# One pool for weights, sums and residual in a hybrid decoder layer, and five steps put elsewhere in the order

## The chip, the cores and the metric

The kernel runs on one core of a Trainium2 chip. The metric is the time of one execution on the device in microseconds; three executions of the kernel before gave a median of 2860.52 us (2858.32 to 2864.68).

## The reference

One decoder layer over 256 tokens of width 2048, all in float32. Shortened:

```
h = x + 1/2 * postN(SwiGLU_1(preN(x)))                  # D_FF = 5632
proj = preN(h) @ w_in  -> q | k | v | z | xBC | dt | gates
A = diff_attention(q, k, v)                             # 8 heads, causal, two softmax maps
S = mamba2(z, conv(xBC), softplus(dt + bias))           # 64 heads in 8 groups, chunks of 128
m = sigmoid(g_A) * (A @ w_branch_att) + sigmoid(g_S) * (S @ w_branch_ssm)
h = h + postN(m @ w_out)
h = h + 1/2 * postN(SwiGLU_2(preN(h)))
```

Every norm is an RMSNorm with a gain. Nearly all the work is products of 256 tokens with weights that are read once.

## The kernel before, in words

Tokens lie as two tiles of 128 (`NT = 2`). A float32 product is made of three matmuls on numbers that are split into a high and a low part: `split` (L109) takes a block of weights `raw`, ScalarE writes the high part `w_hi` (L122), VectorE subtracts it and writes the low part `w_lo` (L123). Activations are split in the same way into a "slot". `matmul3` and `prod` issue x_hi*w_hi, x_hi*w_lo, x_lo*w_hi.

Weights come in slabs of 1 MB, which are 8 KB on each of 128 partitions, on the queue of SyncE. The pool `raws` holds three of them, and `hpool` two further buffers of 8 KB: for the sums `wsum` in the two SwiGLUs, for `xv` and `dec` in the SSD groups, and for the residual `h` at the borders between the sub-layers. `wsplit` holds four high and four low parts of half a slab (and two of a quarter). A tile waits until its buffer's last readers are done.

**gate_up** (L338) makes one 512-wide slab of gate and up for one of the 11 values of `j`, out of eight slabs of weights, in the order `ORDER` or `ORDER_D`. Five of the eight are ordinary: two splits, 24 matmuls. The slabs 2, 4 and 6 (`SP`, from `j = 1` on) go a cheaper way, with 7 products (21 matmuls) in place of 8. That way needs four sums of quarters of the slab, which GpSimd makes (L366 to L369): s0 = r0+r3, s1 = r1+r3, s2 = s0+r1, s3 = s2+r2. They go into a tile `wsum` of their own, so they need no more than the landed slab. Four splits follow: a (quarters 0 and 1), d (quarter 2), b (s0, s1), c (s2, s3), and the products in the order p1 and u0 (from a), g0 (d), p5 and p7 (b), p6 and g1 (c); in the first such slab of a `gate_up`, u0 and g0 come later. After three values of `j` (the last time two), `project` multiplies with `w_down`.

The order on each engine is set when the program is built: a list scheduler simulates the engines and takes, of the ready instructions of an engine, the one of highest priority, which is the place in the program; `tc.high_priority(offset=AHEAD)` moves what it covers 300 places forward. All splits and sums stand under it. So an instruction whose input is late in that simulation lets later ones pass, TensorE's too; on the chip each engine keeps the order that was fixed.

**Borders.** After `w_down` and after `w_out`, `PostNorm.finish` (L271) updates `h` by quarters: token tile 0 at once, tile 1 through the returned `update(c)`. Then `h` is transposed into slots for the next projection. `queue` (filled in `pre_slots` and in the loop around L877) makes the third and fourth split behind a border issue after the first step of `update`.

**dt.** `decays` (L558) is a generator for dt and the decays of the SSM; `tick` runs it one step at a time after each projection. Its first step calls `rb()`, which spreads the row scale over the partitions with a matmul (L244, L245). **Merge.** For each n of `w_att`, the gated sum is transposed into a slot right behind the projection (`merged.append(to_slot(...))`).

Of the kernel before, what the change touches and what calls it, by code (L numbers as in the profile page):

```python
# [39 lines left out]
AHEAD = 300  # L40
# [12 lines left out]
def decoder_layer(ctx: ExitStack, tc: tile.TileContext, x, x_t, cols, rows, post_g, wgu1, wd1, w_in,  # L53
                  w_in_t, w_dt, w_att, w_ssm, w_out, wgu2, wd2, out):
    nc = tc.nc
    E = lambda **k: ctx.enter_context(tc.tile_pool(**k))
    const = E(name="const", bufs=1)
    raws = E(name="raws", bufs=3)
    wsplit = E(name="wsplit", bufs=4)
    slots = E(name="slots", bufs=9)  # L60
    big = E(name="big", bufs=1)
    hpool = E(name="hpool", bufs=2)
    tmp = E(name="tmp", bufs=12)
    small = E(name="small", bufs=4)
    psm = E(name="psm", bufs=8, space=bass.MemoryType.PSUM)
# [18 lines left out]
    h = None  # L84
    col = const.tile([P, NCOL], F32, name="col")
    nc.scalar.dma_start(col, cols)
    raw0 = raws.tile([P, 4, S], F32, name="raw")
    xT = big.tile([P, NP, 2, TT], F32, name="xT", tag="big")
    for b in range(2):
        nc.sync.dma_start(xT[:, b], x_t[b])  # L90
# [13 lines left out]
        nc.gpsimd.tensor_tensor(out=dst, in0=v[:, :k], in1=mhalf[:, :k], op=ALU.pow)  # L104

    loaded = [None]
    queue = []

    def split(raw, shape, parts=1, before=None):  # L109
        one = shape[1:] == [S]  # L110
        hi, lo = (wsplit.tile(shape, F32R, name=f"w_{p}", tag=f"w{p}{'1' if one else ''}", bufs=2 if one else None)
                  for p in ("hi", "lo"))
        k = shape[1] // parts
        with ExitStack() as st:
            st.enter_context(tc.high_priority(offset=AHEAD))
            for i in queue.pop(0) if queue else ():
                st.enter_context(tc.issue_after(i.ins))
            for a in range(0, shape[1], k):
                js = slice(a, a + k)
                if before:  # L120
                    before(js)
                nc.scalar.activation(hi[:, js], raw[:, js], AF.Copy)  # L122
                nc.vector.tensor_tensor(out=lo[:, js], in0=raw[:, js], in1=hi[:, js].bitcast(F32), op=ALU.subtract)  # L123
        return hi, lo
# [7 lines left out]
    def project(xs, w, n, by_token=0):  # L132

        ps = [psm.tile([P, S], F32, name="acc", tag="m") for _ in range(NT)]
        tail = []
        for c in range(len(xs)):
            raw = raws.tile([P, 4, S], F32, name="raw")
            loaded[0] = nc.sync.dma_start(raw, w(n, c))  # L140
            sl = xs[c] = xs[c]() if callable(xs[c]) else xs[c]
            for b in range(2):
                hi, lo = split(raw[:, 2 * b:2 * b + 2], [P, 2, S])
                for jj in range(2):
                    j = 2 * b + jj
                    tail.append((sl, j, hi[:, jj], lo[:, jj], c + j == 0, c == len(xs) - 1 and j == 3))
            if c < len(xs) - by_token:
                for sl_, j, wh, wl, first, last in tail:
                    for t in range(NT):
                        matmul3(ps[t], sl_, j, t, wh, wl, first, last)  # L150
                tail = []
        for t in range(NT):
            for sl_, j, wh, wl, first, last in tail:
                matmul3(ps[t], sl_, j, t, wh, wl, first, last)
        return ps

    def project_t(xs, w, n):

        ps = [psm.tile([P, 2 * TT], F32, name="acc", tag="m") for _ in range(2)]
        for b in range(len(xs)):  # L160
            if b % 2 == 0:
                raw = raws.tile([P, 8, 256], F32, name="raw")
                nc.sync.dma_start(raw, w(n, b // 2))
            hi, lo = split(raw[:, 4 * (b % 2):4 * (b % 2) + 4], [P, 4, 256])
            sl = xs[b].rearrange("p j i t -> p j (i t)")
# [172 lines left out]
    def gate_up(at, w, j, order, sp, rstd, fetch=None, after={}):  # L338
# [17 lines left out]
        for i, p in enumerate(order):  # L356
            raw = fetch(p) if fetch else None
            if raw is None:
                raw = raws.tile([P, 4, S], F32, name="raw")
                nc.sync.dma_start(raw, w[j, p])  # L360
            sl, k0 = at[p]
            if p in sp:

                e = hpool.tile([P, 4, S], F32, name="wsum", tag="h")
                with tc.high_priority(offset=AHEAD):
                    nc.gpsimd.tensor_tensor(out=e[:, 0], in0=raw[:, 0], in1=raw[:, 3], op=ALU.add)  # L366
                    nc.gpsimd.tensor_tensor(out=e[:, 1], in0=raw[:, 1], in1=raw[:, 3], op=ALU.add)
                    nc.gpsimd.tensor_tensor(out=e[:, 2], in0=e[:, 0], in1=raw[:, 1], op=ALU.add)
                    nc.gpsimd.tensor_tensor(out=e[:, 3], in0=e[:, 2], in1=raw[:, 2], op=ALU.add)  # L369
                ah, al = split(raw[:, 0:2], [P, 2, S])  # L370
                dh, dl = split(raw[:, 2], [P, S])
                bh, bl = split(e[:, 0:2], [P, 2, S])
                ch, cl = split(e[:, 2:4], [P, 2, S])
                seq = {"p1": (0, ah[:, 0], al[:, 0]), "u0": (6, ah[:, 1], al[:, 1]), "g0": (1, dh, dl),
                       "p5": (3, bh[:, 0], bl[:, 0]), "p7": (5, bh[:, 1], bl[:, 1]),
                       "p6": (4, ch[:, 0], cl[:, 0]), "g1": (2, ch[:, 1], cl[:, 1])}
                for k in (("p1", "p5", "p7", "p6", "u0", "g0", "g1") if i == units[0] else
                          ("p1", "u0", "g0", "p5", "p7", "p6", "g1")):
                    f, wh, wl = seq[k]
                    prod(k, sl[:, f, 0], sl[:, f, 1], wh, wl)  # L380
            else:
# [18 lines left out]
        out = []  # L400
# [110 lines left out]
    def rb():  # L511
        if not along:
            along.append(spread(rstd))
        return along[0]
# [7 lines left out]
    pending = []  # L522
# [17 lines left out]
        return v  # L540


    raw = raws.tile([P, 16, P], F32, name="raw")
    nc.sync.dma_start(raw, w_dt)
    pdt = psm.tile([P, 2 * TT], F32, name="pdt", tag="m")
    for c in range(2):
# [11 lines left out]
    def decays():  # L558
        dtT = tmp.tile([P, TT], F32, name="dtT", tag="t2")
        nc.scalar.activation(dtT, pdt[:, TT:], AF.Copy)  # L560
        nc.vector.tensor_tensor(out=dtT, in0=pdt[:, :TT], in1=dtT, op=ALU.add)
        nc.vector.tensor_tensor(out=dtT, in0=dtT, in1=rb()[:, 0], op=ALU.mult)
        pdv = psm.tile([P, NT, 64], F32, name="pdv", tag="m")
        for t in range(NT):
            nc.tensor.transpose(pdv[:, t], dtT[0:64, t * P:(t + 1) * P], ident[0:64, 0:64])
        yield
        nega = const.tile([P, 64], F32, name="nega")
        nc.scalar.activation(nega, row[:, 64:128], AF.Exp)
        nc.vector.tensor_scalar_mul(nega, nega, -1.0)
# [19 lines left out]
        nc.vector.scalar_tensor_tensor(out=dt, in0=dt, scalar=2.0, in1=v, op0=ALU.mult, op1=ALU.add)  # L589
        nc.vector.tensor_tensor(out=da, in0=dt, in1=nega.unsqueeze(1).broadcast_to([P, NT, 64]), op=ALU.mult)  # L590
        yield
        pcs = psm.tile([P, NT, 64], F32, name="pcs", tag="m")
        nc.tensor.matmul(pcs, tri, da, start=True, stop=True)
        nc.vector.tensor_copy(acs, pcs)
# [10 lines left out]
        for t in range(NT):  # L605
            nc.gpsimd.dma_start(acsD[t], acsT[:, t])

        yield
        lam = const.tile([P, 2], F32, name="lam")
        for i in range(2):  # L610
            c0 = C_LAM + 2 * i
# [5 lines left out]
        nc.vector.scalar_tensor_tensor(out=lamc, in0=elam[:, 0:1], scalar=LAMBDA_INIT, in1=elam[:, 1:2],  # L617
                                       op0=ALU.add, op1=ALU.subtract)

    pending.append(decays())  # L620
    subg = const.tile([P, 4], F32, name="subg")
    for i in range(2):
        nc.vector.tensor_scalar_mul(subg[:, 2 * i:2 * i + 2], col[:, C_SUB:C_SUB + 2], 1.0 - LAMBDA_INIT)
# [226 lines left out]

    merged, gates = [], {}
    gates[0], gates[1] = gate(W_GA), gate(W_GA + 1)
    for n in range(4):
        ps = project(att, lambda n, c: w_att[n, c], n)
        for t in range(NT):
            a = part[:, t, n * S:(n + 1) * S]
            nc.vector.tensor_tensor(out=gates[n][t], in0=ps[t], in1=gates[n][t], op=ALU.mult)
            nc.vector.tensor_tensor(out=a, in0=a, in1=gates[n][t], op=ALU.add)
        if n + 2 < 4:
            gates[n + 2] = gate(W_GA + n + 2)  # L860
        merged.append(to_slot([part[:, t, n * S:(n + 1) * S] for t in range(NT)]))

    h = [hpool.tile([P, D], F32, name=f"hb{t}", tag="h") for t in range(NT)]
    for t in range(NT):
# [81 lines left out]
```

## Time and profile before

| | before |
|---|---|
| median of three executions | 2860.52 us |
| the profiled execution, its own time | 2859.6 us |
| its span in the trace | 2857.9 us |
| TensorE busy | 2788.2 us, 98% |
| VectorE, ScalarE, GpSimd busy | 2035.1, 1442.8, 601.7 us |
| granted TensorE clock, mean | 0.992 |
| DMA, mean of 16 engines | 189 GB/s, 541.49 MB |

All times below are from this one execution, in microseconds from the start of the span. Matmuls are pipelined: a busy TensorE is not one at its peak, and a row of 512 columns is shown with 0.39 us though the next starts 0.227 us later. A wait for several semaphores is put down to the one that came last.

### The profile page before, as it was taken

The page shows a single profiled execution, that of the slowest core. Times are in us where ns is not written, and L with a number is a line of the kernel's source. Part 1 is how long each engine was busy: PE and PEld are TensorE (multiplying, and loading weights), DVE is VectorE, ACT ScalarE, POOL GpSimd, SP SyncE. Part 2 cuts the span into 40 slices and gives each one's busy share as a digit, 9 for nine tenths or more (in the row PEclk, how much of TensorE's full clock was granted, in tenths as well). Part 3 has the DMA queues.
Part 4 walks back from the last instruction along what each step waited for, and adds up shares of the span by engine and source line. Part 5 has one row for each costly group of instructions (what it writes and reads, how often), then busy time and mean ns, then how long its engine had stood idle before and what let it go on. Part 6 is the DMA issues. An engine that isn't in the chain of part 4 may idle for free. (4 is left out here: it accounts for less than half of the span.)

```text
span 2857.9 us, 33698 instructions
## 1 busy us (share of the span) xinstructions
PE 2788.2 (98%) x13120; PEld 2314.6 (81%) x13120; DVE 2035.1 (71%) x2311; ACT 1442.8 (50%) x1824; POOL 601.7 (21%) x377
## 2 busy tenths in 40 slices
PE   8999999999999999999999999999999999999998
PEld 6887887887778888888788888888878887887877
DVE  7858868778677886777665555545568679688686
ACT  6545545544555555545444444444455455455454
POOL 2415325233011120111100000000005145054150
PEclk9999999999999999999999999999999999999999
DMA  6555555556545554545545445555555554545555
GB/s 239 186 183 191 192 181 204 190 191 232 182 175 182 188 178 176 206 166 189 205 177 177 171 170 182 197 197 187 187 186 189 197 186 180 204 181 207 185 201 183
DMA packets 77984, 541.49 MB, mean 189 GB/s; under 512 B 8768, under 2 KB 8912, under 8 KB 14080
## 3 DMA queue, kind: packets, MB, share of 16 engines
q1 hardware_dynamic: 73152, 519.08, 50.3%
q0 software_dynamic: 4528, 20.09, 2.1%
q8 instruction: 103, 1.69, 0.2%
q14 instruction: 57, 0.47, 0.0%
q10 hardware_dynamic: 144, 0.17, 0.0%
HBM read 532.94 MB, written 6.36 MB: 189 GB/s over the span
## 5 line engine op out<-in xcount | busy, mean ns | idle before, releaser
L123 DVE TENSOR_TENSOR w_lo<-raw,w_hi 128x1024 fp32r<-128x1024 f32 (+1 forms) x978 | 1341.9, 1383 | 704.7 <-ACT w_hi L122 697.9
L122 ACT ACTIVATE w_hi<-raw 128x1024 fp32r<-128x1024 f32 (+1 forms) x978 | 1000.0, 1032 | 1073.6 <-PE acc L130 574.2
L128 PE MATMUL acc<-w_hi,slot 128*128 128x512 f32 x1856 | 731.0, 394 | 0.9 <-DVE y L685 0.3
L129 PE MATMUL acc<-w_lo,slot 128*128 128x512 f32 x1856 | 724.2, 390 | 0.0
L130 PE MATMUL acc<-w_hi,slot 128*128 128x512 f32 x1856 | 721.3, 390 | 0.0
L128 PEld LDWEIGHTS acc<-w_hi,slot 128*128 128x128 f32 x1856 | 349.5, 188 | 77.4 <-ACT slot L185 4.1
L169 PE MATMUL acc<-slot,w_hi 128*128 128x512 f32 x1280 | 408.7, 400 | 0.2 <-ACT zs L729 0.2
L129 PEld LDWEIGHTS acc<-w_lo,slot 128*128 128x128 f32 x1856 | 349.7, 188 | 73.1 <-issue 1.0
L130 PEld LDWEIGHTS acc<-w_hi,slot 128*128 128x128 f32 x1856 | 349.4, 188 | 73.0
L350 PE MATMUL gu<-w_lo,slot 128*128 128x512 f32 x928 | 366.0, 394 | 12.5 <-DVE w_lo L123 12.3
L349 PE MATMUL gu<-w_hi,slot 128*128 128x512 f32 x928 | 365.0, 394 | 7.1 <-ACT w_hi L122 7.1
L351 PE MATMUL gu<-w_hi,slot 128*128 128x512 f32 x928 | 363.0, 391 | 0.0
L171 PEld LDWEIGHTS acc<-slot,w_lo 128*128 128x128 f32 x1280 | 241.3, 189 | 56.4
L366 POOL TENSOR_TENSOR wsum<-raw 128x512 f32<-128x512 f32 x60 | 82.8, 1381 | 862.7 <-DMA raw<-in_wgu 836.3
L171 PE MATMUL acc<-slot,w_lo 128*128 128x256 f32 x1280 | 253.7, 279 | 0.0
L350 PEld LDWEIGHTS gu<-w_lo,slot 128*128 128x128 f32 x928 | 175.2, 189 | 57.6 <-DVE w_lo L123 22.7
L349 PEld LDWEIGHTS gu<-w_hi,slot 128*128 128x128 f32 x928 | 175.4, 189 | 45.8 <-ACT w_hi L122 7.5
L351 PEld LDWEIGHTS gu<-w_hi,slot 128*128 128x128 f32 x928 | 175.1, 189 | 35.9
L169 PEld LDWEIGHTS acc<-slot,w_hi 128*128 128x128 f32 x1280 | 197.5, 189 | 4.3 <-issue 2.4
L122 ACT ACTIVATE w_hi<-wsum 128x1024 fp32r<-128x1024 f32 x120 | 126.7, 1056 | 117.0 <-POOL wsum L369 50.5
L350 PE MATMUL gu<-w_lo,sums 128*128 128x512 f32 x420 | 165.4, 394 | 10.8 <-DVE w_lo L123 10.7
L123 DVE TENSOR_TENSOR w_lo<-wsum,w_hi 128x1024 fp32r<-128x1024 f32 x120 | 158.6, 1342 | 16.8 <-ACT w_hi L122 16.3
(229 smaller groups left out, 2354.5 us busy)
## 6 DMA issues: line engine op xcount, KB each, us to landing
raw<-in_wgu SPq DMA_DIRECT2D x175, 1024.0 KB, 4.8
raw<-in_wd SPq DMA_DIRECT2D x88, 1024.0 KB, 4.7
raw<-in_w_in SPq DMA_DIRECT2D x80, 1024.0 KB, 4.7
raw<-in_w_in_t SPq DMA_DIRECT2D x80, 1024.0 KB, 4.8
raw<-in_w_ssm SPq DMA_DIRECT2D x32, 1024.0 KB, 4.8
raw<-in_w_att SPq DMA_DIRECT2D x16, 1024.0 KB, 4.7
raw<-in_w_out SPq DMA_DIRECT2D x16, 1024.0 KB, 4.8
dec<-acsD POOLq DMA_DIRECT2D x16, 512.0 KB, 5.2
```

The lines of the kernel that those rows point to most:

```text
L122: nc.scalar.activation(hi[:, js], raw[:, js], AF.Copy)
L123: nc.vector.tensor_tensor(out=lo[:, js], in0=raw[:, js], in1=hi[:, js].bitcast(F32), op=ALU.subtract)
L128: nc.tensor.matmul(ps, xh, wh, start=first, stop=False)
L129: nc.tensor.matmul(ps, xh, wl, start=False, stop=False)
L130: nc.tensor.matmul(ps, xl, wh, start=False, stop=last)
L169: nc.tensor.matmul(ps[f], hi[:, j, wf[f]], sl[:, j], start=b + j == 0, stop=False)
L171: nc.tensor.matmul(ps[f][:, TT:], lo[:, j, wf[f]], sl[:, j, :TT], start=False, stop=b == len(xs) - 1 and j == 3)
L349: nc.tensor.matmul(bank[k], xh, wh, start=done[k] == 1, stop=False)
L350: nc.tensor.matmul(bank[k], xh, wl, start=False, stop=False)
L351: nc.tensor.matmul(bank[k], xl, wh, start=False, stop=done[k] == count[k])
L366: nc.gpsimd.tensor_tensor(out=e[:, 0], in0=raw[:, 0], in1=raw[:, 3], op=ALU.add)
```

## The change

`raws` is gone: its slabs come from `hpool`, which has five buffers for slabs, `xv`, `dec` and `h` together. In the slabs 2, 4 and 6 the sums are written over the slab itself, after its splits a and d, and in another order, so that split b reads quarters 0 and 1 again (p5, p6) and split c quarters 2 and 3 (g1, p7). `split` takes no high priority while `queue` holds something, that is for the first four splits behind each border. Of `decays`, the first step runs at once (`next(chain)`), the transposes of dtT come one step later, an empty step stands ahead of the cumulated sums, and the step ahead of lambda is gone. The transposes of the merged slab n come after the projection n+1, those of the last one inside the next projection.

```
-    raws = E(name="raws", bufs=3)
-    hpool = E(name="hpool", bufs=2)
+    hpool = E(name="hpool", bufs=5)
...
-    raw = raws.tile([P, 4, S], F32, name="raw")
+    raw = hpool.tile([P, 4, S], F32, name="raw", tag="h")
...
+    ahead = [AHEAD]
...
-            st.enter_context(tc.high_priority(offset=AHEAD))
+            if ahead[0] and not queue:
+                st.enter_context(tc.high_priority(offset=ahead[0]))
...
-                e = hpool.tile([P, 4, S], F32, name="wsum", tag="h")
-                with tc.high_priority(offset=AHEAD):
-                    nc.gpsimd.tensor_tensor(out=e[:, 0], in0=raw[:, 0], in1=raw[:, 3], op=ALU.add)
-                    nc.gpsimd.tensor_tensor(out=e[:, 1], in0=raw[:, 1], in1=raw[:, 3], op=ALU.add)
-                    nc.gpsimd.tensor_tensor(out=e[:, 2], in0=e[:, 0], in1=raw[:, 1], op=ALU.add)
-                    nc.gpsimd.tensor_tensor(out=e[:, 3], in0=e[:, 2], in1=raw[:, 2], op=ALU.add)
                 ah, al = split(raw[:, 0:2], [P, 2, S])
                 dh, dl = split(raw[:, 2], [P, S])
-                bh, bl = split(e[:, 0:2], [P, 2, S])
-                ch, cl = split(e[:, 2:4], [P, 2, S])
+                with tc.high_priority(offset=AHEAD):
+                    for o, a, b in ((0, 0, 3), (3, 1, 3), (1, 0, 1), (2, 1, 2)):
+                        nc.gpsimd.tensor_tensor(out=raw[:, o], in0=raw[:, a], in1=raw[:, b], op=ALU.add)
+                bh, bl = split(raw[:, 0:2], [P, 2, S])
+                ch, cl = split(raw[:, 2:4], [P, 2, S])
...
-                for k in (("p1", "p5", "p7", "p6", "u0", "g0", "g1") if i == units[0] else
-                          ("p1", "u0", "g0", "p5", "p7", "p6", "g1")):
+                for k in (("p1", "p5", "p6", "p7", "u0", "g0", "g1") if i == units[0] else
+                          ("p1", "u0", "g0", "p5", "p6", "p7", "g1")):
...
         nc.vector.tensor_tensor(out=dtT, in0=dtT, in1=rb()[:, 0], op=ALU.mult)
+        yield
         pdv = psm.tile([P, NT, 64], F32, name="pdv", tag="m")
         for t in range(NT):
             nc.tensor.transpose(pdv[:, t], dtT[0:64, t * P:(t + 1) * P], ident[0:64, 0:64])
-        yield
...
         nc.vector.tensor_tensor(out=da, in0=dt, in1=nega.unsqueeze(1).broadcast_to([P, NT, 64]), op=ALU.mult)
         yield
+        yield
         pcs = psm.tile([P, NT, 64], F32, name="pcs", tag="m")
...
-        yield
         lam = const.tile([P, 2], F32, name="lam")
...
-    pending.append(decays())
+    chain = decays()
+    next(chain)
+    pending.append(chain)
...
+    turn = lambda n: to_slot([part[:, t, n * S:(n + 1) * S] for t in range(NT)])
     for n in range(4):
         ps = project(att, lambda n, c: w_att[n, c], n)
+        if n:
+            merged.append(turn(n - 1))
...
-        merged.append(to_slot([part[:, t, n * S:(n + 1) * S] for t in range(NT)]))
+    merged.append(lambda: turn(3))
```

## Rows read from the trace of the kernel before

**Rows 1.** The page: busy time, share of the span, instructions.

```profile
PE 2788.2 (98%) x13120; PEld 2314.6 (81%) x13120; DVE 2035.1 (71%) x2311; ACT 1442.8 (50%) x1824; POOL 601.7 (21%) x377
```

**Rows 2.** Waits of TensorE, whole span: us in total, times, longest.

```profile
PE gu L350 <- DVE w_lo L123: 23.0, 17, 2.1
...
PE tp L205 <- DVE h L285: 4.2, 2, 2.2
PE tp L881 <- DVE hb L285: 4.0, 2, 2.8
...
PE tp L205 <- DVE part L858: 3.1, 2, 1.6
PE rb L245 <- DVE pre_diag L244: 2.8, 1, 2.8
...
PE pcs L593 <- DVE da L590: 1.7, 1, 1.7
...
PE pdv L565 <- DVE dtT L562: 1.1, 1, 1.1
```

**Rows 3.** Waits of ScalarE, whole span.

```profile
ACT w_hi L122 <- DMA raw<-in_wgu: 121.6, 55, 5.3
```

**Rows 4.** Stages of 41.5, 20, 12 and 519 us: busy times, clock.

```profile
221.00:262.50 41.50, 39.38 (x172) 32.08 (x171) 36.04 (x28) 21.43 (x23) 24.18 (x14) 1.00 0.49 177
...
744.00:764.00 20.00, 13.28 (x60) 10.71 (x59) 17.28 (x26) 14.48 (x33) 4.52 (x3) 0.74 0.56 210
797.00:809.00 12.00, 8.12 (x34) 6.66 (x33) 8.60 (x16) 3.01 (x7) 1.44 (x1) 0.72 0.46 171
...
867.00:1386.00 519.00, 517.29 (x2736) 438.63 (x2734) 396.80 (x614) 288.65 (x382) 88.97 (x56) 1.00 0.52 183
```

**Rows 5.** The sums on GpSimd by line: count, busy us, mean ns, idle before.

```profile
L368 POOL TENSOR_TENSOR wsum<-wsum,raw 128x512 f32<-128x512 f32 x60 | 132.7, 2212 | 0.0
...
L367 POOL TENSOR_TENSOR wsum<-raw 128x512 f32<-128x512 f32 x60 | 107.8, 1797 | 0.0
L366 POOL TENSOR_TENSOR wsum<-raw 128x512 f32<-128x512 f32 x60 | 82.8, 1381 | 862.7 <-DMA raw<-in_wgu 836.3 <-DVE w_lo L123 18.5 <-ACT w_hi L122 7.9
```

**Rows 6.** ScalarE in a gate_up: start, duration, instruction, idle before.

```profile
224.62 1.06 ACT L122 ACTIVATE w_hi<-raw 128x1024 fp32r<-128x1024 f32 x1 [0.30 <-PE gu L351]
...
228.75 1.06 ACT L122 ACTIVATE w_hi<-wsum 128x1024 fp32r<-128x1024 f32 x1 [1.66 <-PE gu L351]
```

**Rows 7.** VectorE in the same stretch.

```profile
220.04 2.31 DVE L123 TENSOR_TENSOR w_lo<-wsum,w_hi 128x1024 fp32r<-128x1024 f32 x1
...
229.84 1.23 DVE L123 TENSOR_TENSOR w_lo<-wsum,w_hi 128x1024 fp32r<-128x1024 f32 x1 [0.75 <-ACT w_hi L122]
```

**Rows 8.** GpSimd there: the first sum of the same slab.

```profile
218.27 1.30 POOL L366 TENSOR_TENSOR wsum<-raw 128x512 f32<-128x512 f32 x1 [3.75 <-DVE w_lo L123]
```

**Rows 9.** TensorE there: the slab's first product, and p5's second matmul.

```profile
231.22 0.39 PE L349 MATMUL gu<-w_hi,sums 128*128 128x512 f32 x1
...
233.48 0.39 PE L350 MATMUL gu<-w_lo,sums 128*128 128x512 f32 x1
```

**Rows 10.** TensorE at the start of j = 1.

```profile
63.56 0.63 PE L351 MATMUL gu<-w_hi,sums 128*128 128x512 f32 x1
63.99 0.63 PE L349 MATMUL gu<-w_hi,slot 128*128 128x512 f32 x1
```

**Rows 11.** VectorE at the first border.

```profile
744.68 4.53 DVE L123 TENSOR_TENSOR w_lo<-raw,w_hi 128x1024 fp32r<-128x1024 f32 x2
749.13 0.68 DVE L469 TENSOR_TENSOR fsum<-acc,f 128x512 f32<-128x512 f32 x1
...
752.09 2.35 DVE L123 TENSOR_TENSOR w_lo<-raw,w_hi 128x1024 fp32r<-128x1024 f32 x2
```

**Rows 12.** TensorE at the same border.

```profile
745.98 0.39 PE L130 MATMUL acc<-w_hi,slot 128*128 128x512 f32 x1
...
757.14 0.77 PE L128 MATMUL acc<-w_hi,slot 128*128 128x512 f32 x1
```

More of the change, by code (lines that the diff above doesn't have):

```diff
@@ L86, in decoder_layer @@
     nc.scalar.dma_start(col, cols)
-    raw0 = raws.tile([P, 4, S], F32, name="raw")
+    raw0 = hpool.tile([P, 4, S], F32, name="raw", tag="h")
     xT = big.tile([P, NP, 2, TT], F32, name="xT", tag="big")
@@ L161, in project_t @@
             if b % 2 == 0:
-                raw = raws.tile([P, 8, 256], F32, name="raw")
+                raw = hpool.tile([P, 8, 256], F32, name="raw", tag="h")
                 nc.sync.dma_start(raw, w(n, b // 2))
@@ L358, in gate_up @@
             if raw is None:
-                raw = raws.tile([P, 4, S], F32, name="raw")
+                raw = hpool.tile([P, 4, S], F32, name="raw", tag="h")
                 nc.sync.dma_start(raw, w[j, p])
@@ L362, in gate_up @@
             if p in sp:
-                e = hpool.tile([P, 4, S], F32, name="wsum", tag="h")
-                with tc.high_priority(offset=AHEAD):
-                    nc.gpsimd.tensor_tensor(out=e[:, 0], in0=raw[:, 0], in1=raw[:, 3], op=ALU.add)
-                    nc.gpsimd.tensor_tensor(out=e[:, 1], in0=raw[:, 1], in1=raw[:, 3], op=ALU.add)
-                    nc.gpsimd.tensor_tensor(out=e[:, 2], in0=e[:, 0], in1=raw[:, 1], op=ALU.add)
-                    nc.gpsimd.tensor_tensor(out=e[:, 3], in0=e[:, 2], in1=raw[:, 2], op=ALU.add)
                 ah, al = split(raw[:, 0:2], [P, 2, S])
                 dh, dl = split(raw[:, 2], [P, S])
-                bh, bl = split(e[:, 0:2], [P, 2, S])
-                ch, cl = split(e[:, 2:4], [P, 2, S])
+                with tc.high_priority(offset=AHEAD):
[3 more added lines that the diff above has]
+                ch, cl = split(raw[:, 2:4], [P, 2, S])
                 seq = {"p1": (0, ah[:, 0], al[:, 0]), "u0": (6, ah[:, 1], al[:, 1]), "g0": (1, dh, dl),
-                       "p5": (3, bh[:, 0], bl[:, 0]), "p7": (5, bh[:, 1], bl[:, 1]),
-                       "p6": (4, ch[:, 0], cl[:, 0]), "g1": (2, ch[:, 1], cl[:, 1])}
-                for k in (("p1", "p5", "p7", "p6", "u0", "g0", "g1") if i == units[0] else
-                          ("p1", "u0", "g0", "p5", "p7", "p6", "g1")):
+                       "p5": (3, bh[:, 0], bl[:, 0]), "p6": (4, bh[:, 1], bl[:, 1]),
+                       "g1": (2, ch[:, 0], cl[:, 0]), "p7": (5, ch[:, 1], cl[:, 1])}
+                for k in (("p1", "p5", "p6", "p7", "u0", "g0", "g1") if i == units[0] else
+                          ("p1", "u0", "g0", "p5", "p6", "p7", "g1")):
                     f, wh, wl = seq[k]
@@ L540, in proj_in_t @@
         return v
-    raw = raws.tile([P, 16, P], F32, name="raw")
+    raw = hpool.tile([P, 16, P], F32, name="raw", tag="h")
     nc.sync.dma_start(raw, w_dt)
```

## The prediction

> **What bounds the kernel now.** I read the page first. TensorE is busy for 2788.2 of 2857.9 us [rows 1]; the reader is to see that at most the other 69.7 us, and what a lowered clock costs, are to be had. So the next view is TensorE's waits [rows 2]: 23.0 us in 17 waits of the SwiGLUs for a low part of weights, four rows at the borders and the merge (4.2, 4.0, 3.1 us), and three around dt (2.8, 1.7, 1.1 us). The stages then say where no gain lies: from 867 to 1386 us, most of the SSD part, TensorE is busy for 517.29 of 519.00 us at full clock, while the stretch around the first border has 13.28 of 20.00 us at a mean clock of 0.74 and that around dt 8.12 of 12.00 at 0.72 [rows 4]. Last I follow one slab of the SwiGLU through the four engines [rows 5 to 9], because there the change alters what waits for what.
>
> The kernel is bound by TensorE's stream of matmuls, and the change leaves every matmul in it. It can win only idle time and clock, and it can lose wherever a split comes later than its matmul.
>
> **Sums in place.** Nothing is computed less: 60 slabs with four sums each [rows 5], the same splits. What changes is the order of events in a slab. Before, the sums started as the slab landed (218.27) [rows 8], 12.95 us ahead of the slab's first product (231.22) [rows 9], and ran while the engines did older splits. After, s0 overwrites quarter 0, which split a reads, so no sum can start before a's low part is written. Split a can't come much earlier than now: at 224.62 it waited for TensorE to give back a buffer of `wsplit` [rows 6], of which there are four as before. Two more buffers for slabs don't help there.
>
> So the chain from 224.62 is: a high 1.06, a low 1.23, three sums (s0, s1, s2: b needs quarters 0 and 1) at 1.30 each, b high 1.06, b low 1.23 [rows 6 to 8], and five hand-offs. One hand-off is read from 228.75 + 1.06 = 229.81 to 229.84, 0.03 us [rows 6, 7]; I take 0.05. That makes 8.48 + 0.25 = 8.73 us, and b's low part is there at 233.35. TensorE needs it at 233.48 [rows 9]. The margin is 0.13 us if nothing gets in between.
>
> Something will. A low part took 2.31 us where sums ran and 1.23 where none did [rows 7], and the sums' means are 1.38, 1.80 and 2.21 us [rows 5], together 5.39 in place of 3.90. With those the chain is 1.49 us longer, 1.36 us past the margin. But the slab's own low parts no longer run beside its sums, they stand ahead and behind; what can still meet them is the ordinary slabs' 10 of the 22 low parts that a gate_up has (5 ordinary slabs with two, 3 with four). 10/22 of 1.49 is 0.68 us, less the margin 0.55 us for each slab, and for 60 slabs 33 us. That is the value I take. The bounds: 60 x 1.36 = +82 us if they meet as often as now; at the other end nothing, if TensorE does other products meanwhile, less the 23 us of waits for low parts [rows 2] in case earlier loads cure these.
>
> The Trainium skill, "SBUF — State Buffer", section "SBUF: two separate sides", says that VectorE with two SBUF inputs and a GpSimd operation that reads SBUF exclude each other through a shared pair of ports, held for the whole instruction, and that the loser blocks. The trace agrees: 2.31 us for a low part beside sums against 1.23 alone [rows 7]. By that rule each low part that falls among the three sums costs the chain about one low part, 1.23 us, an estimate that lies under the 1.49 above; by plain sharing of bandwidth with room to spare it would cost nothing, and the sum would be that of rival 1.
>
> **What waits behind the new waits.** On GpSimd the sums now wait for VectorE; behind them stand the loads of `post_g` and `h`, which are wanted many matmuls later, so I cost this at nothing; without that cover it is one sum, 1.3 us, a few times. On ScalarE the high part of b waits for sums, and the next ordinary slab's high parts may stand behind it; they are wanted at least 2.7 us later (12 matmuls), so what is late next is b itself, costed above.
>
> **One pool.** ScalarE waited 121.6 us in 55 waits for slabs of the SwiGLUs to land [rows 3]. Five buffers will take most of these away, but hardly any reaches TensorE, whose waits there are nearly all for low parts [rows 2]. I cost it at nothing beside the -23 us of the lower bound. In the SSD part `xv` and `dec` leave three buffers for slabs, as now; TensorE's 1.7 us of idle time in 519 [rows 4] cover nothing more, so if a load has to queue behind them it is a loss, at most one landing wait for each of 8 groups (121.6/55 = 2.2 us, 18 us in all). I take 0.
>
> **Borders.** At the first border the last matmul ends at 745.98 + 0.39 = 746.37 [rows 12], but `fsum` for tile 1 starts at 749.13, because two low parts hold VectorE for 4.53 us from 744.68 [rows 11]: 2.76 us. Two more, 2.35 us from 752.09 [rows 11], stand ahead of the later steps of `update`. Full use would be 5.1 us of the 10.8 us from 746.37 to the first product at 757.14 [rows 12]. The splits have to be made somewhere, though, and that product's second matmul needs one, so I take the first part and a third of the second, 3.5 us, and for the two borders, which have like waits [rows 2], -7 us. Bounds: -10 us, and +5 us if the four splits (2.35 us a pair at each border) come wholly behind.
>
> **dt.** Running the first step at once puts the row scale's matmul behind the products of dt, and the transposes and the cumulated sums one step after their inputs. The three waits are 2.8 + 1.1 + 1.7 = 5.6 us [rows 2]. The stretch at a clock of 0.72 [rows 4] follows them; 12 us at 0.72 with part idle hold a few us of slowed matmuls, of which I count 1.4 back: -7 us. Bounds: 0 and -10 us. The moved steps are short VectorE work of the same count.
>
> **Merge.** Two waits, 3.1 us [rows 2], go when the transposes come a whole projection later; the last slab is wanted as the fourth of the next projection. -3 us, bounds 0 and -3.
>
> **The sum.** +33 - 7 - 7 - 3 = +16 us on the profiled execution's 2859.6 us: 2875.6 us. Its own time lies 0.9 us under the median, so as a median about 2876 us, slower by 0.5%.
>
> **Rivals.**
> 1. *TensorE takes other products while b is late, and the change is faster.* At the start of `j = 1` the products of slab 2 (`sums`) ran ahead of those of slab 0 (`slot`), which comes first in the program's order there [rows 10]: the scheduler does fill TensorE out of order. With five buffers the next ordinary slab has landed. For it speaks that a gate_up of 183 matmuls of 0.227 us takes 41.5 us, of which VectorE is busy only 36.04 and GpSimd 24.18 [rows 4]; against it, that the order is fixed on simulated times and that four `wsplit` buffers keep it short. Price: FFN term 0, so 2860.5 - 17 = 2843 us. The point from which it decides: if the 60 slabs lose less than 0.28 us each (17/60), the change isn't slower.
> 2. *The two nearly cancel.* FFN +11 to +23 us: within 0.2%, about 2861 us. 0.2% is 5.7 us, about what a measurement of this kernel can tell from no change.
> 3. *VectorE and GpSimd become the bound of the SwiGLUs.* Nineteen low parts of 1.23 and three of half that make 25.2 us; twelve sums at 1.30 make 15.6; 40.8 of 41.5 us [rows 4, 7, 8] if they never overlapped. Today they are spread over the gate_up, after the change they crowd between the first and the third of the slabs 2, 4, 6. For it: the margin of 0.13 us; against it: a gate_up holds 41.5 us with that work already. Price: the upper bound, +82 - 10 = 2932 us; half of it, 2897 us, is the likelier form.
> 4. *Clock.* A stall in the SwiGLUs may bring the clock down as at the border (0.74 [rows 4]); that is part of 3.
>
> **Chances.** Forecast (slower, 2866 to 2890) 0.41; rival 1 0.35; rival 2 0.13; rival 3 0.11. Faster by over 0.2% 0.35, within 0.14, slower 0.51 (the edge of rival 2 leans to slower). The forecast's own range is 2866 to 2890 us; for 8 in 10 the range takes in rival 1 down to 2838 us and rival 3 up to 2902 us.
>
> **What would show it.** Right: TensorE's waits for b's low part (line of `prod`'s second matmul, tile `sums`), some 30 us more than now; GpSimd's sums waiting for VectorE's low parts in place of DMA; the 121.6 us of ScalarE gone or turned into waits for the sums; no waits at the transposes of `part`, `rb`, `pdv`, `pcs`; `fsum` at the border right behind its matmuls. Wrong: if TensorE's stream shows ordinary products between p1 and p5 without idle time, the sums cost nothing and rival 1 holds; if the border's first product comes no earlier, the splits there were needed.

## The result, and the profile after

The changed kernel takes 2951.49 us (median of 4 runs, 2950.64 to 2953.58), the kernel before 2861.32 us (4 runs, 2858.32 to 2864.68): a ratio of 1.0316, 95% interval 1.0298 to 1.0334. It is slower, as forecast, but by 90 us and not by 16, and 49 us above the end of the range, 2902 us. The profiled execution has a span of 2948.9 us, 91.0 more than before.

TensorE first: the page's row, then its waits over the whole span (us in total, times, longest).

```profile
PE 2825.9 (96%) x13120; PEld 2327.1 (79%) x13120; DVE 1872.0 (63%) x2311; ACT 1433.5 (49%) x1822; POOL 498.8 (17%) x377
```

```profile
PE gu L350 <- ACT w_hi L123: 28.3, 20, 7.0
PE gu L351 <- DVE w_lo L124: 27.4, 39, 0.9
PE acc L172 <- DVE w_lo L124: 21.8, 5, 5.0
PE acc L130 <- DVE w_lo L124: 10.4, 4, 4.8
PE acc L129 <- ACT w_hi L123: 7.2, 3, 3.5
PE acc L170 <- ACT w_hi L123: 5.5, 5, 3.5
...
PE tp L206 <- DVE h L286: 1.9, 1, 1.9
```

Lines have moved by one. The same 13120 matmuls are busy 37.7 us longer than in [rows 1]. About 27 us of that can be clock, an estimate from the mean granted clock of 0.983 over 2948.9 us against 0.992 over 2857.9; the rest comes of how a row is shown, 0.39 us long with the next start after 0.227, so that each new stop adds up to 0.16 us of busy time. The four rows of `acc` are new: 17 waits of the mixer's projections, 44.9 us together, of a kind that [rows 2] do not have at all. The rows of `part`, `pdv` and `pcs` are gone.

Where the time went can be cut at two marks, the first transposition of `h` (first border) and of `hb` (second border). Here is the view by tile, `tp`, of before and of after; the last times are the start of the first and of the last of the 32 transpositions.

```profile
L205 PE MATMUL tp<-ident,h x32: 270/417/476, 746.2 to 761.9; 128*128 128x128 f32 x32
L881 PE MATMUL tp<-ident,hb x32: 270/273/473, 2110.0 to 2123.3; 128*128 128x128 f32 x32
```

```profile
L206 PE MATMUL tp<-ident,h x32: 271/417/476, 765.8 to 779.7; 128*128 128x128 f32 x32
L885 PE MATMUL tp<-ident,hb x32: 271/342/474, 2177.0 to 2187.1; 128*128 128x128 f32 x32
```

The first SwiGLU grows from 746.2 to 765.8 us (+19.6), the mixer with the first border from 1363.8 to 1411.2 (+47.4), the second border with the second SwiGLU from 747.9 to 771.9 (+24.0). Half of the loss lies in the mixer, where the prediction had only gains.

**The mixer.** Columns as in [rows 4]: a stall, the SSD part, the first border, dt.

```profile
925.00:945.00 20.00, 14.58 (x61) 11.35 (x61) 12.09 (x27) 8.22 (x10) 2.56 (x2) 0.78 0.19 78
872.00:1446.00 574.00, 527.18 (x2691) 442.69 (x2690) 393.61 (x609) 286.26 (x378) 102.60 (x56) 0.95 0.45 162
763.00:783.00 20.00, 15.39 (x72) 12.61 (x72) 18.23 (x28) 15.85 (x36) 4.52 (x3) 0.83 0.41 158
803.00:815.00 12.00, 11.02 (x65) 9.41 (x64) 6.34 (x10) 5.27 (x7) 0.00 (x0) 1.00 0.46 167
```

Where TensorE was idle for 1.7 us in 519 [rows 4], it is now idle for 46.8 in 574, at a mean granted clock of 0.95. One stall from near, ScalarE (four rows), VectorE (three), TensorE (two), and the loads on SP's queue:

```profile
920.72 1.06 ACT L123 ACTIVATE w_hi<-raw 128x1024 fp32r<-128x1024 f32 x1 [1.66 <-PE acc L131]
930.92 1.37 ACT L730 ACTIVATE zs<-acc,pre_rstd 128x512 f32<-128x512 f32 x2 [9.14 <-PE acc L131]
...
936.21 3.88 ACT L123 ACTIVATE w_hi<-raw 128x1024 fp32r<-128x1024 f32 x4
```

```profile
921.81 1.23 DVE L124 TENSOR_TENSOR w_lo<-raw,w_hi 128x1024 fp32r<-128x1024 f32 x1 [1.50 <-ACT w_hi L123]
932.46 0.69 DVE L697 TENSOR_TENSOR yo<-pyo,din 128x512 f32<-128x512 f32 x1 [9.42 <-PE pyo L695]
...
939.43 2.36 DVE L124 TENSOR_TENSOR w_lo<-raw,w_hi 128x1024 fp32r<-128x1024 f32 x2
```

```profile
937.30 1.22 PE L170 MATMUL acc<-slot,w_hi 128*128 128x512 f32 x2 [3.45 <-ACT w_hi L123]
...
940.71 0.80 PE L172 MATMUL acc<-slot,w_lo 128*128 128x256 f32 x2 [1.97 <-DVE w_lo L124]
```

```profile
909.62 0.33 SPq L164 DMA_DIRECT2D raw<-in_w_in_t  x1
...
917.63 0.33 SPq L164 DMA_DIRECT2D raw<-in_w_in_t  x1
```

The next projection's first two slabs are issued at 909.62 and 917.63; a slab's load lands 4.8 us after its issue (the page's median), so both are there by about 922.5. Yet ScalarE splits none of them: from 921.78 to 930.92 it waits for the z projection's matmuls to end, because `zs` (the gate of z) stands ahead of those splits in its order. VectorE waits 9.42 us in the same way at `yo`. Both are idle with the work beside them, and TensorE, some 2.5 us of small matmuls after the end of z, runs dry. No load is late here; the splits are, by the order of the instructions. ScalarE's wait at `zs` is 59.5 us in 7 times over the span.

**The SwiGLUs.** The sums wait for split a, as foreseen, and hardly meet low parts:

```profile
L370 POOL TENSOR_TENSOR raw<-raw 128x512 f32<-128x512 f32 x240 | 322.8, 1345 | 1022.9 <-DVE w_lo L124 1008.7
```

```profile
ACT w_hi L123 <- POOL raw L370: 337.9, 119, 6.3
...
ACT w_hi L123 <- DMA raw<-in_wgu: 51.2, 32, 3.4
```

A mean of 1.35 us stands against 1.38 to 2.21 [rows 5]. ScalarE's 121.6 us of waits for slabs [rows 3] are 51.2, but it now stands 337.9 us at the high parts of sums. One slab, the second with sums in its gate_up (GpSimd, ScalarE, VectorE, TensorE):

```profile
269.11 6.08 POOL L370 TENSOR_TENSOR raw<-raw 128x512 f32<-128x512 f32 x4 [8.76 <-DVE w_lo L124]
```

```profile
273.87 1.06 ACT L123 ACTIVATE w_hi<-raw 128x1024 fp32r<-128x1024 f32 x1 [6.33 <-POOL raw L370]
```

```profile
274.96 3.71 DVE L124 TENSOR_TENSOR w_lo<-raw,w_hi 128x1024 fp32r<-128x1024 f32 x3 [3.63 <-ACT w_hi L123]
```

```profile
271.33 0.39 PE L350 MATMUL gu<-w_hi,sums 128*128 128x512 f32 x1
...
273.14 0.39 PE L352 MATMUL gu<-w_hi,sums 128*128 128x512 f32 x1
274.98 0.51 PE L350 MATMUL gu<-w_hi,sums 128*128 128x512 f32 x1 [1.45 <-ACT w_hi L123]
276.32 0.50 PE L351 MATMUL gu<-w_lo,sums 128*128 128x512 f32 x1 [0.84 <-DVE w_lo L124]
...
277.38 0.63 PE L352 MATMUL gu<-w_hi,sums 128*128 128x512 f32 x1
277.81 0.63 PE L350 MATMUL gu<-w_hi,sums 128*128 128x512 f32 x1
```

TensorE does p1, u0 and g0 from 271.33 and stands twice at p5: for b's high part, then for its low part. Behind the two stops the granted clock is 0.50, the lower level of 1.2 GHz, from 277.3 to 280.7 us: eight matmuls start 0.43 us apart in place of 0.23. So the listed waits are not the whole price. In the two SwiGLUs together TensorE's idle time grows by 19.6 us (50.9 to 70.5) and its busy time, for the same matmuls, by 24.0.

The page's rows of `prod`'s second matmul on `sums`, before and after, and of its first after:

```profile
L350 PE MATMUL gu<-w_lo,sums 128*128 128x512 f32 x420 | 165.4, 394 | 10.8 <-DVE w_lo L123 10.7
```

```profile
L351 PE MATMUL gu<-w_lo,sums 128*128 128x512 f32 x420 | 176.7, 421 | 27.6 <-DVE w_lo L124 26.8
L350 PE MATMUL gu<-w_hi,sums 128*128 128x512 f32 x420 | 171.5, 408 | 22.6 <-ACT w_hi L123 21.2
```

Each half of the loss has its own chain, so the experiments take them one by one.

### The profile page after: what moved, and what is told of

The parts are those of the page before. It is cut to its first block, busy times and chain, and to the rows that moved or that the text cites. A ratio compares the mean times of both kernels' runs of the same rounds, so it can differ in the third digit from the quotient of the medians.

```text
span 2948.9 us, 33745 instructions
## 1 busy us (share of the span) xinstructions
PE 2825.9 (96%) x13120; PEld 2327.1 (79%) x13120; DVE 1872.0 (63%) x2311; ACT 1433.5 (49%) x1822; POOL 498.8 (17%) x377
## 3 DMA queue, kind: packets, MB, share of 16 engines
q1 hardware_dynamic: 73152, 519.08, 48.7%
## 5 line engine op out<-in xcount | busy, mean ns | idle before, releaser
L124 DVE TENSOR_TENSOR w_lo<-raw,w_hi 128x1024 fp32r<-128x1024 f32 (+1 forms) x1098 | 1325.0, 1222 | 928.9 <-ACT w_hi L123 919.7
L123 ACT ACTIVATE w_hi<-raw 128x1024 fp32r<-128x1024 f32 (+1 forms) x1098 | 1115.2, 1033 | 1257.8 <-PE acc L131 549.3
L370 POOL TENSOR_TENSOR raw<-raw 128x512 f32<-128x512 f32 x240 | 322.8, 1345 | 1022.9 <-DVE w_lo L124 1008.7
L351 PE MATMUL gu<-w_lo,sums 128*128 128x512 f32 x420 | 176.7, 421 | 27.6 <-DVE w_lo L124 26.8
L350 PE MATMUL gu<-w_hi,sums 128*128 128x512 f32 x420 | 171.5, 408 | 22.6 <-ACT w_hi L123 21.2
L352 PE MATMUL gu<-w_hi,sums 128*128 128x512 f32 x420 | 169.8, 404 | 0.0
```

Of the source, the lines that this page charges most:

```text
L350: nc.tensor.matmul(bank[k], xh, wh, start=done[k] == 1, stop=False)
L351: nc.tensor.matmul(bank[k], xh, wl, start=False, stop=False)
L352: nc.tensor.matmul(bank[k], xl, wh, start=False, stop=done[k] == count[k])
L370: nc.gpsimd.tensor_tensor(out=raw[:, o], in0=raw[:, a], in1=raw[:, b], op=ALU.add)
```

## The experiments

All times are medians in us. Each ratio is to runs of the kernel before that were made beside it; their medians were 2859.5 to 2863.2. The three stages are cut at the same two marks as above, in the profiled execution of each kernel.

| kernel | time | ratio to before (95%) | first SwiGLU | mixer | second SwiGLU |
|---|---|---|---|---|---|
| before | 2861.3 | | 746.2 | 1363.8 | 747.9 |
| changed | 2951.5 | 1.0298 to 1.0334 | 765.8 | 1411.2 | 771.9 |
| e1 small parts | 2843.5 | 0.9921 to 0.9954 | 745.7 | 1347.9 | 746.4 |
| e2 one pool | 2928.7 | 1.0210 to 1.0247 | 748.8 | 1424.9 | 750.9 |
| e3 in place | 2915.7 | 1.0172 to 1.0203 | 773.6 | 1362.4 | 777.3 |
| e4 two pools | 2897.3 | 1.0107 to 1.0137 | 772.7 | 1348.9 | 773.6 |
| e5 four buffers | 2958.0 | 1.0321 to 1.0352 | 769.5 | 1410.9 | 775.1 |
| e6 early touch | 2893.6 | 1.0093 to 1.0127 | 766.5 | 1353.2 | 772.9 |
| e7 two sums ahead | 2999.9 | 1.0467 to 1.0499 | 791.4 | 1413.0 | 795.0 |
| e10 four sums ahead | 2978.8 | 1.0393 to 1.0424 | 780.4 | 1410.6 | 786.1 |
| e11 a sum fewer | 2876.6 | 1.0035 to 1.0065 | 728.4 | 1410.8 | 735.1 |
| e8 five in wsplit | 2933.2 | 1.0233 to 1.0263 | 756.5 | 1408.5 | 764.1 |
| e9 touch, five in wsplit | 2873.8 | 1.0026 to 1.0055 | 757.9 | 1349.6 | 764.5 |
| e12 sums ahead, touch, five | 2831.6 | 0.9878 to 0.9908 | 737.6 | 1349.3 | 740.3 |
| e13 second half later | 2902.8 | 1.0135 to 1.0165 | 743.2 | 1410.9 | 746.9 |
| e14 only splits later | 2947.8 | 1.0288 to 1.0323 | 765.3 | 1412.9 | 769.2 |
| e15 e13 and touch | 2846.9 | 0.9938 to 0.9968 | 743.3 | 1352.9 | 748.6 |
| e16 e15, five in wsplit | 2823.4 | 0.9861 to 0.9890 | 735.9 | 1349.8 | 741.3 |

### Which part costs: e1 to e4

e1 is the kernel before with the border, dt and merge edits alone; e2 is the kernel before with its pools joined; e3 with the sums in place alone; e4 is the changed kernel with two pools again. The edit of e4:

```
-    hpool = E(name="hpool", bufs=5)
+    raws = E(name="raws", bufs=3)
+    hpool = E(name="hpool", bufs=2)
...
-            raw = hpool.tile([P, 4, S], F32, name="raw", tag="h")
+            raw = raws.tile([P, 4, S], F32, name="raw")
```

Expected of e1: 

> The kernel before with only the border, dt and merge edits; two pools (3 + 2 buffers) and sums in a tile of their own as before. Theory A (the new waits of TensorE in the SSD part come of the one pool): these parts do what the prediction costed, about -17 us, so 2844 us (2840 to 2850), and no waits for split weights in the SSD part. Theory B (they come of the order: the dt chain's later turns, the splits without priority): the SSD part loses its 50 us here too, so 2861 - 17 + 50 = 2894 us.

Expected of e2: 

> The kernel before with only its two pools joined to one of five buffers; sums still in a tile of their own, taken from that pool. Theory A: the SSD part loses about 50 us, so 2911 us (2900 to 2925, the SwiGLUs may move by some us either way), with TensorE waiting for split weights in projections once per SSD group. Theory B: 2861 us, no such waits.

Expected of e3: 

> The kernel before with only the sums made in place, 3 + 2 buffers as before (the pool of two is then empty in the SwiGLUs). Theory C (the later sums cost time by their own chain, whatever the pool): about +45 us, 2906 us (2890 to 2920), waits at p1 and p5 as in the changed kernel. Theory D (the loss in the SwiGLUs comes of the shared pool too): within 15 us of 2861 us.

Expected of e4: 

> The changed kernel with slabs in a pool of three and xv, dec, h in one of two, as before; all else changed. Theory A: the 50 us of the SSD part come back, 2901 us (2885 to 2910), and there are no new waits in projections. Theory B: no gain, about 2950 us. With C its SwiGLUs stand as slow as in the changed kernel; with D they are as fast as before and the time falls to about 2850 us.

Measured against before: e1 -18.6, e2 +66.5, e3 +53.6, e4 +35.1 us. The small parts and the sums add up (-18.6 + 53.6 = 35.0). The stages part the causes cleanly: with one pool the mixer takes 61 to 63 us longer (e2 against before, changed against e1) and no other edit does that; the sums in place lengthen both SwiGLUs and nothing else. Theories A and C stand, B and D fall; e2 lies 4 us above the 2925 that A allowed: the mixer lost 61 us where 50 were expected, and the SwiGLUs 5.6. One pool also gives something: with the sums in place the two SwiGLUs together are 8.6 us shorter with five buffers than with three (changed against e4).

### Why one pool costs: e5 and e6

Theory A has two forms. e5 has four buffers in place of five. e6 keeps five, takes `xv` and `dec` ahead of the z projection, and writes one element of `xv` there:

```
+        xv = hpool.tile([P, 4, S], F32, name="xv", tag="h")
+        dec = hpool.tile([P, NT, 8, P], F32, name="dec", tag="h")
+        nc.vector.memset(xv[:, 0, 0:1], 0.0)
+        ssd = ssd_group(g, xc, bct[g], zs, xv, dec)
-        ssd = ssd_group(g, xc, bct[g], zs)
         if g < 7:
             zs = z_silu(proj_in(W_Z + g + 1))
```

Expected of e5: 

> The changed kernel with four buffers in its one pool in place of five. Theory A1 (too few buffers: in the SSD part the slabs land too late because xv and dec hold buffers): a buffer fewer makes the stalls there longer, 2990 us or more. Theory A2 (order: the instructions' order is fixed when the kernel is built, buffers of a pool are handed out in the program's order, and the splits of the next projection are put behind work that waits for the z projection's last matmul, although their slabs are there): the SSD part is as slow as with five, 2951 us (2943 to 2965), and the SwiGLUs decide the rest.

Expected of e6: 

> The changed kernel with xv and dec taken from the pool ahead of the z projection and one element of xv set to zero there (it is overwritten later), so that xv's buffer is handed out before those of the slabs behind it. Still one pool of five. Theory A1: no gain, 2951 us or a little more, since xv holds its buffer longer. Theory A2: the SSD part's 50 to 54 us come back, 2899 us (2885 to 2912).

A buffer fewer leaves the mixer as it was (1410.9 against 1411.2), so a want of buffers it is not. Taking `xv` and `dec` earlier, with one element written there, takes 58 us out of it (1353.2). ScalarE in e6 around the same z projection, and TensorE's stage:

```profile
919.67 1.06 ACT L123 ACTIVATE w_hi<-raw 128x1024 fp32r<-128x1024 f32 x1 [1.67 <-PE acc L131]
922.38 1.06 ACT L123 ACTIVATE w_hi<-raw 128x1024 fp32r<-128x1024 f32 x1 [1.65 <-PE acc L131]
925.05 1.06 ACT L123 ACTIVATE w_hi<-raw 128x1024 fp32r<-128x1024 f32 x1 [1.61 <-PE acc L131]
...
927.42 1.27 ACT L728 ACTIVATE zs<-acc,pre_rstd 128x512 f32<-128x512 f32 x2
```

```profile
905.00:945.00 40.00, 40.00 (x209) 33.71 (x208) 31.83 (x53) 23.00 (x30) 7.75 (x4) 1.00 0.56 210
```

The splits go on until `zs`, paced only by the buffers of `wsplit` that TensorE gives back, and TensorE does not stop at all. That is theory A2: the order of the instructions is made when the kernel is built; in the changed kernel `xv` is written for the first time behind the z projection, and the slabs that follow it in the program, which now come from the same pool, are not counted on before that. How the builder reasons is in no trace; that taking the tiles earlier with this write decides, and not the number of buffers, the two runs show. No run has the one without the other, so whether the early place or the write does it stays open.

### Why the late sums cost: e7, e10, e11, e8, e9

e7, e10 and e11 change which sums stand ahead of split b, and e11 leaves the third sum out. In all three some product reads a quarter that is not its sum, so they do not compute the layer; the matmuls and the splits are the same. In the changed kernel three sums stand ahead:

```
 changed  (0, 0, 3), (3, 1, 3), (1, 0, 1), (2, 1, 2)   then b, c
 e7       (0, 0, 3), (3, 1, 3)   then b, then (1, 0, 1), (2, 1, 2), then c
 e10      (0, 0, 3), (3, 1, 3), (2, 1, 2), (1, 0, 1)   then b, c
 e11      (0, 0, 3), (3, 1, 3), (2, 1, 2)   then b, c
```

Expected of e7: 

> The changed kernel with two sums ahead of split b and two behind it, in place of three and one (the quarter that p6 reads is then not its sum). Same work on every engine. Theory C1 (the chain a, sums, b is longer than TensorE's lead): the chain is one sum, 1.3 us, shorter for 60 slabs, of which most stall by more than that; 2951 - 30 = 2921 us (2900 to 2935). Theory C2 (VectorE and GpSimd are crowded, rival 3 of the prediction): within 6 us of 2951 us.

Expected of e10: 

> The changed kernel with all four sums ahead of split b (the third and the fourth change places, so the quarter that p7 reads takes p6's before its sum). Same work on every engine. Theory C1: the chain is one sum, 1.3 us, longer for each of 60 slabs, nearly all of it stalls: 2951 + 65 = 3016 us (2995 to 3032). Theory C2: within 6 us of 2951 us.

Expected of e11: 

> The changed kernel without the third sum (what p6 reads is then not summed, and p7's sum lacks a term): two sums ahead of split b, the last beside it, so that the chains to b and to c are both one sum shorter; GpSimd has 60 sums of 1.35 us fewer. Theory C1: up to 1.3 us for each of 60 slabs, where the stall is that long; 2951 - 40 = 2911 us (2898 to 2930). Theory C2 in its last form (GpSimd's work, not the chain): 0 to 10 us.

e7 went the other way, +48.4 us, and the expectation was careless: the third sum writes a quarter that split b reads, so it now waits for b, and c waits for two more sums; the whole chain a, sums, b, sums, c grew. e10 lost 27.3 us where 65 were expected: b comes a sum later, but c is ready with it. e11 gained 74.9 us, where at most 53 were expected. Its edit does more than its expectation says: b now reads only one quarter that is a sum, so it waits for one sum in place of three, and c for three in place of four. GpSimd's and ScalarE's rows of one slab, first in the changed kernel (b starts 4.04 us after the first sum), then in e11 (1.32 us):

```profile
254.99 5.37 POOL L370 TENSOR_TENSOR raw<-raw 128x512 f32<-128x512 f32 x4 [10.81 <-DVE w_lo L124]
259.03 1.06 ACT L123 ACTIVATE w_hi<-raw 128x1024 fp32r<-128x1024 f32 x1 [5.92 <-POOL raw L370]
```

```profile
245.52 2.66 POOL L370 TENSOR_TENSOR raw<-raw 128x512 f32<-128x512 f32 x2 [1.16 <-DVE w_lo L124]
246.84 1.06 ACT L123 ACTIVATE w_hi<-raw 128x1024 fp32r<-128x1024 f32 x1 [4.91 <-POOL raw L370]
```

The gain is also more than the SwiGLUs had lost: they are 28.6 us shorter than those of e1 (1463.5 against 1492.1). What the 60 sums fewer gave and what the shorter chain was not taken apart. TensorE's waits in e11:

```profile
PE gu L351 <- DVE w_lo L124: 8.8, 16, 0.9
```

27.4 us became 8.8, and the 28.3 us at high parts 7.0, which is one wait at the program's start. The engines' work is the same in e7 and e10 as in the changed kernel; only the order differs, and the time moves by 27 to 48 us. Theory C2, that crowding is the cause and the order is worth at most 6 us, falls.

e8 and e9 give the 8 KB of a pool buffer to `wsplit` (five buffers), e9 with the touch of e6; e12 does so with the sums ahead in a tile of their own.

Expected of e8: 

> The changed kernel with the 8 KB of one pool buffer given to the split weights: four buffers in the pool (2958 us with that alone, the run with four buffers) and five in wsplit. Theory C1 (the chain a, sums, b starts when TensorE gives a wsplit buffer back, and is longer than the lead that four buffers give): one buffer more starts a earlier by one split's products, 6 to 12 matmuls of 0.227 us, 1.4 to 2.7 us, against stalls of 1 to 2.8 us; some 40 of the SwiGLUs' 54 us come back, 2918 us (2903 to 2932), with the SSD part as slow as before it. Theory C3 (ScalarE's queue: it stands 306 us at the high parts of sums, and what is behind it comes late, whatever the depth): within 8 us of 2958 us.

Expected of e9: 

> The changed kernel with one element of xv set to zero ahead of the z projection, four buffers in the pool and five in wsplit. Theories A2 and C1 together: 54 us of the SSD part and some 40 us of the SwiGLUs come back, 2861 us (2845 to 2878). A2 with C3: about 2902 us. If two buffers for slabs beside xv and dec are too few, the SSD part stalls for loads and it stays above 2880 us with C1.

Expected of e12: 

> The border, dt and merge edits with sums in a tile of their own as before; one pool of four, one element of xv set to zero ahead of the z projection, five buffers in wsplit. With the sums made ahead, what is left in the SwiGLUs is 23 us of waits for low parts; one more wsplit buffer may take half of them: 2833 us (2825 to 2850) against 2844 us with the three edits alone. If a pool of four is too tight for slab, sum, xv and dec: slower than 2844 us.

e8 gains 24.8 us on e5, 15 less than expected and three times what C3 allows; e9 another 59.5 us by the touch. With the sums ahead, e12 is at 2831.6 us, 12 us below e1.

### Chain or queue: e13 to e16

e13 puts b, c and their four products behind the ordinary slab that follows; e14 moves only the splits and leaves b's and c's products ahead of the ordinary slab's. In both, u0 and g0 also come ahead of p5 in the first such slab of a `gate_up`, where the changed kernel has them last. e15 is e13 with the touch, e16 is e15 with four buffers in the pool and five in `wsplit`.

```
+                def rest(raw=raw, sl=sl):
+                    bh, bl = split(raw[:, 0:2], [P, 2, S])
+                    ch, cl = split(raw[:, 2:4], [P, 2, S])
...
+                late = rest
...
                             prod(f"{kind}{t}", xh, xl, wh[:, q], wl[:, q])
+                if late:
+                    late()
+                    late = None
```

In e14 the three lines of `late` stand ahead of the ordinary slab's loop of products, behind its two splits.

Expected of e13: 

> The changed kernel with the second half of each sums slab (splits b and c and their four products) put behind the splits and products of the ordinary slab that follows. Sums still in place, one pool of five. Theory C1 (TensorE has no product left between g0 and p5): 24 matmuls of the ordinary slab, 5.4 us, now cover the chain; the SwiGLUs' 54 us come back, 2897 us (2885 to 2912). Theory C3 (ScalarE's queue): the ordinary slab's high parts stand ahead of b's as well, so it gains too, about the same; the next run tells the two apart.

Expected of e14: 

> As the run before it, but TensorE's order stays that of the changed kernel (p1, u0, g0, p5, p6, p7, g1, then the ordinary slab): only the splits of the ordinary slab go ahead of b's and c's on ScalarE and VectorE. Theory C3: ScalarE does the ordinary slab while the sums run, 30 to 54 us come back, 2908 us (2895 to 2925). Theory C1: TensorE has still nothing to do between g0 and p5, and b waits for a wsplit buffer or a slab more: no gain, 2951 to 2985 us.

Expected of e15: 

> The second half of each sums slab behind the ordinary slab, and one element of xv set to zero ahead of the z projection; sums in place, one pool of five. If the two causes account for the whole loss, what is left is the gain of the border, dt and merge edits, 18.6 us: 2843 us (2835 to 2855). If something third costs time in the changed kernel, it stays above 2860 us.

Expected of e16: 

> As the run before it with four buffers in the pool and five in wsplit. With the chain covered, a fifth wsplit buffer has less to give than the 25 us it gave without: 2833 us (2823 to 2845), against 2831.6 us of the run with sums in a tile of their own and five in wsplit. If four buffers are too tight with the longer life of a sums slab: slower than 2845 us.

e13 gains 48.7 us, e14 3.7, a little more than the nothing that C1 gave it. ScalarE's waits for the sums, first in e14, then in e13, and the sums of e13:

```profile
ACT w_hi L123 <- POOL raw L370: 107.4, 59, 3.4
```

```profile
ACT w_hi L123 <- POOL raw L370: 216.6, 85, 6.1
```

```profile
L370 POOL TENSOR_TENSOR raw<-raw 128x512 f32<-128x512 f32 x240 | 425.4, 1773 | 889.3 <-DVE w_lo L124 875.2
```

e14 frees ScalarE's queue most and wins next to nothing, probably since b is then behind two more splits; e13 frees it less and wins all, with 24 more matmuls for TensorE to do meanwhile. So it is the chain that TensorE could not cover (C1). And the sums are slower in the faster kernel, 1.77 us against 1.35. e15 comes to 2846.9 us: with both causes taken out, the SwiGLUs are within 2 us of before in sum (1491.9 against 1494.1) and the mixer is 5.0 us longer than e1's; apart from these 5 us, which stay unexplained, nothing third is left. e16, with the one pool and the sums in place, has the lowest median of this study, 2823.4 us (2822.0 to 2829.1), 1.3% under the kernel before; the interval of its ratio overlaps with that of e12, so the two cannot be told apart.

## Why the prediction was wrong, point by point

**One pool, 0.** This step failed, and with it the size of the whole. Its sentence was that "in the SSD part xv and dec leave three buffers for slabs, as now", with at most 18 us if a load has to queue. The count of buffers was right and beside the point: loads were in time, and e5 with fewer buffers loses no more. What the step left out is that joining the pools also changed the order of the instructions: the four splits that ran ahead of `zs` fell behind it, and e6 brought them back. That `xv`, first written behind the z projection, now stood in the slabs' line is the likely reason; no trace shows the builder's reasoning. Price: 63.3 us (changed against e1). TensorE's idle time is 46.8 us in the SSD window against 3.3 us in e1's (545 us, of which 541.66 busy); a matmul takes 0.1959 us there on average against 0.1901 in e1, for 2691 of them some 16 us, most of it lowered clock (mean granted clock 0.95 there, 1.00 in e1's). No rival named it.

**Sums in place, +33.** The chain and its sign were right, the size was too small, and what gave the +33 was wrong: without the contention, which hardly came (below), the prediction's own sum leaves nothing past the margin, so that 33 lies as near as it does is partly luck. Measured: +53.6 us with the pools as before (0.89 us a slab, 0.55 were costed), and about 46 us in the changed kernel, whose five buffers help (its SwiGLUs take 1537.7 us against 1492.1 in e1). The bound of +82 held. The term that was mis-sized is the start: the chain was counted from a wsplit buffer's return, which would start the sums 4.2 us ahead of p1 (224.62 + 2.39 to 231.22, [rows 6, 9]). In the slab above they start at 269.11, 2.2 us ahead of p1 at 271.33. There split a's low part stands in VectorE's queue behind others and behind the end of a gate_up. The three sums and the hand-offs take 4.76 us (269.11 to 273.87), 4.05 were counted. 2.0 + 0.7, less the margin of 0.13, is 2.6 us; the two waits of p5 are 2.3. Why split a starts late in each slab was not taken apart further. The prediction also took all 60 slabs alike, while in the first of each `gate_up`, 20 of the 60, p5 follows p1 directly, six matmuls or 1.4 us sooner; what that cost was not measured apart.

The contention that the +33 rested on hardly came: in the changed kernel a sum takes 1.35 us on average, and 1.30 were counted without any. The Trainium skill, "SBUF — State Buffer", section "SBUF: two separate sides", says that a VectorE operation with two SBUF inputs and a GpSimd operation that reads SBUF exclude each other. The trace agrees in so far as sums are longer where more of them meet low parts (1.77 us in e13), and e13 is still 49 us faster. Such meetings did not set the time of the changed kernel.

**Borders -7, dt -7, merge -3.** Together -17, measured -18.6 (e1). That the total is so close is partly luck: in e1's trace the two borders give 4.3 us (14.5 and 10.2 us from first to last transposition, against 15.7 and 13.3), where 7 were counted, and the mixer without its border 14.7, where dt and merge were to give 10. The waits of `part`, `pdv` and `pcs` are gone and that of `rb` falls from 2.8 to 1.0 us. The stretch around dt has 11.02 of 12 us at full clock, where [rows 4] had 8.12 at 0.72. At the border one half was misjudged: `fsum` is not right behind its matmuls,

```profile
764.24 4.52 DVE L124 TENSOR_TENSOR w_lo<-raw,w_hi 128x1024 fp32r<-128x1024 f32 x2
768.69 0.68 DVE L468 TENSOR_TENSOR fsum<-acc,f 128x512 f32<-128x512 f32 x1
```

it stands behind two low parts as in [rows 11]. What was won is the other pair, which stood between the steps of `update`. From first to last transposition the borders of the changed kernel take 13.9 and 10.1 us: -5.0.

**The rivals.** Rival 1 (TensorE takes other products) did not happen by itself; e13 had to write it into the program, and then it was worth 48.7 us, as that rival's reason said. Rival 3 came near in size by chance (2932 as its upper price) but not in cause: VectorE is busy for less of the span (63%, before 71%) and the sums run faster. Rival 4, the clock, came in the SwiGLUs (0.50 behind the stops of the slab above), and in the SSD part too, where it had not been named. Of the signs, TensorE's waits for b's low part were to be "some 30 us more than now"; they rose by 16.1 us (10.7 to 26.8, the page's rows on `sums`), about half, and 21.2 us at high parts, which no sign named, came beside them.

## What to carry to other kernels

Joining buffer pools changes more than counts: a tile that is written late can hold back the tiles behind it, and the order in which splits, copies and gates are put on each engine may change in a stage that nobody edited; look for an engine idle beside work whose input has landed, and try to take the late tile earlier, with one element written, before counting buffers. When a step is made to wait for an earlier one, add up the whole chain to the last reader, every queue in it included, and ask what the bounding engine does meanwhile; giving it the next unit's matmuls was worth 48.7 us here, and clearing ScalarE's queue 3.7. Cost a part in every stage that shares its resource, not only in the stage it was written for.

## What was not expected of the hardware

In all kernels with the stalls of the SSD part the mean granted clock there is 0.95, though TensorE stops for only some 6 us at a time. In the 20 us around the stall shown above TensorE is idle for 5.4 us and the mean is 0.78, between its two levels of 2.4 and 1.2 GHz: TensorE runs dry at about 933.9 us, and from 936.1 to 946.3 us the granted clock is 0.50. About a quarter of the mixer's 63.3 us is slower matmuls, not idle time. And a stop need not be long: the SwiGLU's stops of 1.45 and 0.84 us, one soon after the other, stand ahead of 3.4 us at the lower level, though only some eight such stretches lie in the two SwiGLUs with their 60 slabs.
